# Rotary rotation of queries and keys in place, with one scratch tile in place of two

## The chip, the cores and the metric

One core of a Trainium2 chip runs the kernel. The metric is the device time of one launch in microseconds (us), the median of several. The engines are named as in the profile: PE multiplies matrices, DVE (vector), ACT (activation) and POOL (GpSimd) work element by element, SP issues transfers (DMA) from one queue, in order. PEld is the loading of PE's weights. Each engine runs its own instructions in program order, so an instruction that waits holds up all that stands behind it on its engine.

## What is computed

A backbone of two layers over 512 latent and 256 context tokens, width 1024. In each layer one input projection feeds three groups of heads: differential attention (queries and keys of 32 values per head), grouped-query attention (6 query and 2 key heads of 64) and a bidirectional gated DeltaNet with chunks of 64. An output projection and a SwiGLU follow. The change is in the rotation of the latent tokens' queries and keys, which the reference writes so:

```
def apply_axial_rope(x, cos, sin):
    xr = x.reshape(shp[0], shp[1], -1, 2, 2, nf).astype(jnp.float32)
    x1, x2 = xr[..., 0, :], xr[..., 1, :]
    c, s = cos[:, None], sin[:, None]
    out = jnp.stack([x1 * c - x2 * s, x2 * c + x1 * s], axis=-2)
```

In the DeltaNet each chunk needs the inverse of a triangular matrix (`lax.linalg.triangular_solve` in the reference). The kernel inverts 32x32 blocks element by element and puts them together with matmuls.

## The kernel before

The kernel is Python code that emits one program. A scheduler then decides in which order each engine runs its instructions, by a simulation of its own of when each would be ready; only the data dependences and the tiles' buffers are fixed. So an edit at one place can move instructions at others. An order that the code gives (`EARLY`, `PLAN` below) sets how the simulation ranks them.

Each layer begins with a projection stage. For groups of 128 tokens PE makes a product (`tps`), ACT copies it from PSUM to a slot of SBUF, and the elementwise engines work on it there. Three names matter: `gk` (a slot with the grouped-query keys and values, "kv", or queries, "gq"), `dq` (a slot with the queries and keys of the differential heads) and `rt` (scratch of the rotation; the profile calls both scratch slots of before `rt`). `rope` is called for each of the 4 latent tiles of kv, gq and dqk in both layers, 24 times: DVE multiplies by the cosine, POOL multiplies the two swapped halves by the sine (two instructions), DVE adds. All of `gk`, `gsq`, `dq`, `rt` take slots of 512 columns from one pool with 6 slots in layer 0 and 5 in layer 1:

```
PROJS = (6, 5)
EARLY = ("0 1 2 5 4 v0 q v1 3 p0 p1 q q v2",
         "0 1 2 v0 5 v1 3 q p0 4 q p1 v2 q")
INV_DVE = ((0,), (0, 2))
```

`EARLY` is the order of the code in this stage: a number prepares one tile of the DeltaNet, `q` is one of kv, gq, dqk, `vN` one inversion (`gdn_invert`, L726), `pN` what follows it for a tile (`gdn_post`, L784). An inversion is a chain of 60 small instructions on `Yg` and `Tg`, each of which needs the one before; `INV_DVE` says which run on DVE (v0 in both layers, v2 in layer 1), the others run on POOL. It loads `Yg` from `Bdram` and stores the result to `Ydram`. `gdn_post` loads that as `Z`, DVE transposes it (`ZT`), and PE merges the blocks (`mg`, L810 and L820) and goes on with `wps` and `ups`. These loads and stores stand in SP's queue, and so do the stores of the rotated tiles (`dqk<-dq`) and their loads for the attention (`gk<-dkv` and others).

Then come the mixers: attention (`S` is the score product, `nm` the row maximum on DVE, `P` the exponential on ACT, `pt` and `PT` its transpose, `pv` the product with the values), together with the DeltaNet's steps (`scan`, `ops`; `kdec` is a factor of theirs made on POOL) and further `p` stages, in the order that a table `PLAN` gives (it begins with "s0 s1 a0 a1 p2 s2" in layer 0). `gqs` and `gks` are the transposed queries and keys, `exp` the PE product that turns them. `wlo` is the rest that a weight leaves after rounding, made on DVE for the weights of a projection.

Of the kernel before, what the change touches and what calls it, by code (L numbers as in the profile page):

```python
# [94 lines left out]
class Net:  # L95
# [894 lines left out]
    def rope(self, out, x, nh, cos, sin, nf):  # L990

        d = 4 * nf
        tmp = self.slot("rt")
        tv = tmp[:, :nh * d].rearrange("p (h d) -> p h d", d=d)
        self.mul(tv, x, cos.unsqueeze(1).to_broadcast([128, nh, d]))
        t4 = self.slot("rt2")[:, :nh * d].rearrange("p (h a s f) -> p h a s f", h=nh, a=2, s=2)
        x4 = x.rearrange("p h (a s f) -> p h a s f", a=2, s=2)
        s4 = sin.rearrange("p (a s f) -> p a s f", a=2, s=2)
        for half in range(2):
            self.mul(t4[:, :, :, half], x4[:, :, :, 1 - half],  # L1000
                     s4[:, :, half].unsqueeze(1).to_broadcast([128, nh, 2, nf]), self.g)
        self.add(out, tv, t4.rearrange("p h a s f -> p h (a s f)"))

    def attn_proj(self, l):
        d = self.dram
# [568 lines left out]
def shape_consts():  # L1574
# [28 lines left out]
    for j, at in enumerate(((0, 1), (2, 3), (0, 2), (1, 3))):  # L1603
        for b in at:
            pick[:, :, j, b] = np.eye(32, dtype=f)
    return {"ident": np.eye(128, dtype=f), "pick": pick.reshape(128, 512), "masks": masks.reshape(128, 768), "mloc": mloc,
            "negm": np.concatenate([negm.reshape(128, 128), masks[:, 2:4].reshape(128, 256)], 1), "blk2": blk2,
            "rope_d": rope(32), "rope_g": rope(64)}

def layout(inp):  # L1610
# [55 lines left out]
```

## Time and profile before

| what | value |
|---|---|
| time, median of 3 runs | 2184.11 us (2183.25 to 2184.77) |
| time of the profiled execution | 2187.43 us |
| its span, first to last instruction | 2185.6 us |
| mean granted clock of PE | 0.943 of full speed |
| busy: PE, DVE, ACT, POOL | 2020.9, 1325.2, 823.8, 525.0 us |

The profiled execution took 3.3 us more than the median, and 1.8 us of its time lie outside the span. Two stretches hold the projection stages with the rotations and the start of the mixers: 190 to 420 us (layer 0) and 1390 to 1600 us (layer 1). The long stretches between are projections and the SwiGLU.

### The profile page before, as it was taken

How to read it: one execution, taken by the hardware profiler on the slowest of the kernel's cores; microseconds unless marked ns; L12 is line 12 of the kernel's file. 1: busy time of each engine (PE TensorE's matmuls, PEld its weight loads, DVE VectorE, ACT ScalarE, POOL GpSimd, SP SyncE). 2: the span in 40 equal slices, each digit the busy share in tenths (PEclk: the TensorE clock that was granted, in tenths of full speed). 3: DMA queues.
4: the chain of work that ended last, by engine and by line, in shares of the span. 5: the costliest groups of instructions: out<-in, count | busy, mean ns of one | idle time of the engine just before them, and what ended most of it. 6: DMA issues, size and time to landing. Idle time of an engine off the chain costs nothing. (4 is left out here: it accounts for less than half of the span.)

```text
span 2185.6 us, 36979 instructions
## 1 busy us (share of the span) xinstructions
PE 2020.9 (92%) x14786; PEld 1672.6 (77%) x14786; DVE 1325.2 (61%) x2223; ACT 823.8 (38%) x1609; POOL 525.0 (24%) x768
## 2 busy tenths in 40 slices
PE   7999877998889999999999989977899799999998
PEld 3788766776668888888888888865676598888887
DVE  6755774575845747565757457687767664443444
ACT  5433315464744321212122344423475653222223
POOL 2403579331014100000000350367323030000002
PEclk9999987698999999999999989987798999999999
DMA  8354434221062324343424411444212242222321
GB/s 296 121 176 132 156 109 113 47 73 35 26 227 78 116 87 154 110 131 102 155 91 140 134 56 48 133 127 125 51 47 60 86 165 77 100 85 92 106 98 61
DMA packets 167596, 236.46 MB, mean 108 GB/s; under 512 B 75328, under 2 KB 109248, under 8 KB 167424
## 3 DMA queue, kind: packets, MB, share of 16 engines
q10 hardware_dynamic: 46160, 144.92, 20.2%
q1 hardware_dynamic: 121264, 89.18, 13.4%
q8 instruction: 116, 1.90, 0.3%
q14 instruction: 56, 0.46, 0.1%
HBM read 198.00 MB, written 36.04 MB: 107 GB/s over the span
## 5 line engine op out<-in xcount | busy, mean ns | idle before, releaser
L185 ACT ACTIVATE whi<-raw 128x1024 fp32r<-128x1024 f32 (+4 forms) x246 | 220.7, 912 | 499.6 <-PE dps L188 207.3
L161 DVE TENSOR_TENSOR wlo<-raw,whi 128x1024 fp32r<-128x1024 f32 (+4 forms) x236 | 250.1, 1074 | 222.1 <-ACT whi L185 221.3
L188 PE MATMUL gu<-ahi,wlo 128*128 128x512 f32 x672 | 264.0, 393 | 1.1 <-DVE wlo L161 1.1
L188 PE MATMUL gu<-ahi,whi 128*128 128x512 f32 x672 | 263.6, 392 | 0.0
L188 PE MATMUL dps<-acth,whi 128*128 128x512 f32 (+1 forms) x560 | 186.6, 348 | 0.4 <-DVE h L179 0.2
L188 PE MATMUL dps<-acth,wlo 128*128 128x512 f32 (+1 forms) x560 | 185.7, 346 | 0.0
L188 PE MATMUL gu<-alo,whi 128*128 128x512 f32 x672 | 168.9, 392 | 0.0
L179 DVE SCALAR_TENSOR_TENSOR junk<-adaw,cb 128x1024 bf16<-128x1024 f32 x112 | 136.8, 1222 | 37.6 <-DMA adaw<-ada_t 36.6
L188 PEld LDWEIGHTS gu<-ahi,wlo 128*128 128x128 f32 x672 | 126.5, 188 | 28.3 <-DVE wlo L161 1.5
L188 PE MATMUL tps<-whi,ahi 128*128 128x512 f32 (+4 forms) x368 | 137.9, 379 | 11.1 <-ACT dq L185 7.2
L188 PEld LDWEIGHTS gu<-alo,whi 128*128 128x128 f32 x672 | 126.3, 188 | 27.6
L179 DVE SCALAR_TENSOR_TENSOR h<-dps,md,h 128x512 f32<-128x512 f32 (+1 forms) x128 | 80.6, 633 | 109.6 <-PE dps L188 109.3
L188 PEld LDWEIGHTS gu<-ahi,whi 128*128 128x128 f32 x672 | 126.5, 188 | 26.7
L188 PE MATMUL tps<-wlo,ahi 128*128 128x512 f32 (+4 forms) x368 | 138.3, 376 | 2.6 <-DVE wlo L161 2.4
L161 POOL TENSOR_TENSOR md<-md,adab 128x2 f32<-128x2 f32 x56 | 32.0, 572 | 439.5 <-DVE junk L179 439.5
L188 PE MATMUL tps<-whi,alo 128*128 128x512 f32 (+4 forms) x368 | 137.3, 373 | 0.0
L1161 DVE TENSOR_REDUCE nm<-S 128x1 f32<-128x768 f32 (+1 forms) x140 | 117.0, 844 | 32.6 <-PE S L188 31.4
L182 ACT ACTIVATE P<-S,nm 128x768 f32<-128x768 f32 (+1 forms) x140 | 114.0, 815 | 51.7 <-DVE nm L1161 46.1
L161 POOL TENSOR_TENSOR sqc<-sqc 128x256 f32<-128x256 f32 x35 | 35.4, 1012 | 397.8 <-ACT sqc L182 397.4
L188 PE MATMUL dps<-actl,whi 128*128 128x512 f32 (+1 forms) x560 | 124.3, 346 | 0.0
L188 PEld LDWEIGHTS dps<-acth,whi 128*128 128x128 f32 x560 | 105.4, 188 | 15.6 <-DVE h L179 0.4
L188 PEld LDWEIGHTS dps<-acth,wlo 128*128 128x128 f32 x560 | 105.7, 189 | 14.3
(295 smaller groups left out, 4629.0 us busy)
## 6 DMA issues: line engine op xcount, KB each, us to landing
raw<-w_u ACTq DMA_DIRECT2D x88, 512.0 KB
adaw<-ada_t ACTq DMA_DIRECT2D x56, 512.0 KB
adaw<-ada_p ACTq DMA_DIRECT2D x24, 512.0 KB
raw<-w_o ACTq DMA_DIRECT2D x24, 512.0 KB
raw<-w_d ACTq DMA_DIRECT2D x44, 256.0 KB
raw<-w_d ACTq DMA_DIRECT2D x32, 320.0 KB
adaq<-ada_q SPq DMA_DIRECT2D x16, 512.0 KB
raw<-w_t ACTq DMA_DIRECT2D x16, 512.0 KB
```

Of the source, the lines that this page charges most:

```text
L161: (eng or self.v).tensor_tensor(out=out, in0=a, in1=b, op=op)
L179: self.v.scalar_tensor_tensor(out=out, in0=a, scalar=sc, in1=b, op0=op0, op1=op1, **k)
L182: self.s.activation(out=out, in_=in_, func=func, **k)
L185: self.s.activation(out=out, in_=in_, func=AF.Copy, **k)
L188: self.t.matmul(out, lhsT, rhs, start=start, stop=stop)
L1161: self.v.tensor_reduce(out=nm, in_=pin, axis=AX.XY if nk == 768 else AX.X, op=ALU.max, negate=True)
```

## The change

`rope` takes one scratch slot. POOL writes its two sine products there first. Then DVE multiplies x by the cosine in place and adds the scratch to it. The instructions are as many as before, of the same shapes. As the cosine product overwrites what POOL reads, it now has to wait for both POOL instructions; before, it could run ahead of them or beside them.

```diff
     def rope(self, out, x, nh, cos, sin, nf):
         d = 4 * nf
-        tmp = self.slot("rt")
-        tv = tmp[:, :nh * d].rearrange("p (h d) -> p h d", d=d)
-        self.mul(tv, x, cos.unsqueeze(1).to_broadcast([128, nh, d]))
-        t4 = self.slot("rt2")[:, :nh * d].rearrange("p (h a s f) -> p h a s f", h=nh, a=2, s=2)
+        t4 = self.slot("rt")[:, :nh * d]
+        tv = t4.rearrange("p (h a s f) -> p h a s f", h=nh, a=2, s=2)
         x4 = x.rearrange("p h (a s f) -> p h a s f", a=2, s=2)
         s4 = sin.rearrange("p (a s f) -> p a s f", a=2, s=2)
         for half in range(2):
-            self.mul(t4[:, :, :, half], x4[:, :, :, 1 - half],
+            self.mul(tv[:, :, :, half], x4[:, :, :, 1 - half],
                      s4[:, :, half].unsqueeze(1).to_broadcast([128, nh, 2, nf]), self.g)
-        self.add(out, tv, t4.rearrange("p h a s f -> p h (a s f)"))
+        self.mul(x, x, cos.unsqueeze(1).to_broadcast([128, nh, d]))
+        self.add(out, x, t4.rearrange("p (h d) -> p h d", d=d))
```

With it the scheduler orders the projection stages and the mixers of both layers anew. Three places follow. A row is a line of the kernel, the operation, output and inputs, its size, and how many of the kind follow one another; numbers behind a name tell tiles apart.

PE, layer 0, before: the attention's first products and then the merge of the DeltaNet's tile 2 (p2), whose first rows are the last two.

```order
L188 MATMUL S<-gks,gqs 128x256 x2
L191 MATMUL pv<-ident,OTs 128x128
L191 MATMUL pt<-ident,P 128x128 x6
L188 MATMUL pv<-PT,gV 64x128 x6
L191 MATMUL pt<-ident,P 128x128 x3
L188 MATMUL pv<-PT,gV 64x128
L188 MATMUL S<-gks,gqs 128x256 x2
L188 MATMUL pv<-PT,gV 64x128 x5
L191 MATMUL exp<-ident,dq 128x128 x2
L810 MATMUL mg_3697<-ZT,Boff 32x32
L810 MATMUL mg_3697<-Z,Boff 32x32
```

The same place of the change:

```order
L191 MATMUL pt<-ident,P 128x128 x6
L188 MATMUL S<-gks,gqs 128x384 x8
L188 MATMUL pv<-PT,gV 64x128 x12
L191 MATMUL pt<-ident,P 128x128 x3
L810 MATMUL mg_3685<-ZT,Boff 32x32
L810 MATMUL mg_3685<-Z,Boff 32x32
```

Between the first `S` of this attention and the merge stood 38 `S`, 36 `pt`, 36 `pv` with values and 2 `exp`; now 20 `S`, 15 `pt` and 12 `pv` stand there. The other 18 `S`, 21 `pt` and 24 `pv` stand behind the merge's first rows. DVE's `ZT` and ACT's copies of this merge moved with it.

POOL, layer 0, before: the two inversions v1 (its last sizes, 96x84, 96x58 and 96x30) and v2 (its middle, 96x238 and 96x240), taken in turns, and the factors `kdec` between them.

```order
L161 TENSOR_TENSOR Yg<-Yg,Tg 96x17x14
L161 TENSOR_TENSOR Tg<-Yg 96x84
L161 TENSOR_TENSOR kdec<-tokm,sufb 64x384
L161 TENSOR_TENSOR kdec<-ident,gl 64x384
L161 TENSOR_TENSOR kdec<-tokm,sufb 64x384
L161 TENSOR_TENSOR kdec<-ident,gl 64x384
L161 TENSOR_TENSOR Tg<-Yg 96x240
L161 TENSOR_TENSOR Yg<-Yg,Tg 96x3x28
```

The same place of the change, down to the end of v1:

```order
L161 TENSOR_TENSOR Yg<-Yg,Tg 96x17x14
L161 TENSOR_TENSOR Yg<-Yg,Tg 96x3x28
L161 TENSOR_TENSOR Tg<-Yg 96x240
L161 TENSOR_TENSOR Tg<-Yg 96x58
L161 TENSOR_TENSOR Yg<-Yg,Tg 96x16x15
L161 TENSOR_TENSOR Yg<-Yg,Tg 96x2x29
L161 TENSOR_TENSOR Tg<-Yg 96x240
L161 TENSOR_TENSOR Tg<-Yg 96x30
L161 TENSOR_TENSOR Yg<-Yg,Tg 96x15x16
L161 TENSOR_TENSOR Yg<-Yg,Tg 96x30
L161 TENSOR_TENSOR Tg<-Yg 96x238
L161 TENSOR_TENSOR kdec<-tokm,sufb 64x384
```

Four `kdec` that stood ahead of v1's last instructions stand behind them.

DVE, layer 1, before: the last scaling of keys and queries, then the start of the inversion v2 (`MEMSET Yg`).

```order
L161 TENSOR_TENSOR gqs<-exp,gqs 64x512
L741 MEMSET Yg 96x32
L161 TENSOR_TENSOR Tg<-Yg 96x30
L161 TENSOR_TENSOR Yg<-Yg,Tg 96x30
L161 TENSOR_TENSOR Tg<-Yg 96x58
L161 TENSOR_TENSOR gqs<-exp,gqs 64x512
L161 TENSOR_TENSOR Yg<-Yg,Tg 96x29x2
L1161 TENSOR_REDUCE nm<-S 128x1
L161 TENSOR_TENSOR Tg<-Yg 96x84
L796 STREAM_TRANSPOSE ZT<-Z 128x768
```

The same place of the change:

```order
L161 TENSOR_TENSOR gqs<-exp,gqs 64x512 x2
L796 STREAM_TRANSPOSE ZT<-Z 128x768
L1160 TENSOR_REDUCE nm<-S 128x1
L741 MEMSET Yg 96x32
L161 TENSOR_TENSOR Tg<-Yg 96x30
L1160 TENSOR_REDUCE nm<-S 128x1
```

The second `gqs` and the transpose of p1 now stand ahead of v2's first instructions.

## Rows read from the trace of the kernel before

**Rows 1.** The page's first part: busy us, share of the span, instructions.

```profile
PE 2020.9 (92%) x14786; PEld 1672.6 (77%) x14786; DVE 1325.2 (61%) x2223; ACT 823.8 (38%) x1609; POOL 525.0 (24%) x768
```

**Rows 2.** Windows: length, then busy us of each engine, granted clock, DMA share, GB/s.

```profile
350.00:400.00 50.00, 45.95 (x652) 36.42 (x646) 25.24 (x52) 22.18 (x56) 36.82 (x65) 0.86 0.32 74
380.00:390.00 10.00, 10.00 (x126) 8.18 (x125) 1.09 (x3) 3.78 (x10) 3.17 (x9) 0.52 0.26 55
700.00:1250.00 550.00, 550.00 (x3160) 484.90 (x3161) 336.32 (x539) 127.24 (x203) 52.92 (x76) 1.00 0.37 122
1450.00:1500.00 50.00, 36.89 (x238) 28.39 (x242) 39.31 (x69) 8.23 (x19) 39.82 (x55) 0.83 0.35 110
1500.00:1550.00 50.00, 35.35 (x541) 27.91 (x540) 42.33 (x87) 24.00 (x56) 28.80 (x46) 0.80 0.53 133
```

**Rows 3.** The tile `rt`: durations in ns (least/median/most); idle us and times ahead of it.

```profile
L161 POOL TENSOR_TENSOR rt<-gk,ropeq x16: 587/804/3227, 255.1 to 1466.0; 128x192 f32<-128x192 f32 x16
...
L161 DVE TENSOR_TENSOR rt<-gk,ropek x8: 285/288/414, 203.2 to 1418.5; 128x128 f32<-128x128 f32 x8
L161 DVE TENSOR_TENSOR rt<-gk,ropeq x8: 542/544/952, 256.1 to 1458.3; 128x384 f32<-128x384 f32 x8
L161 DVE TENSOR_TENSOR rt<-dq,rope_d x8: 675/686/2559, 302.6 to 1495.2; 128x512 f32<-128x512 f32 x8
...
  POOL rt L161: 12.0, 13
```

**Rows 4.** Timeline of DVE, layer 1: start, us, instruction, idle before it and its releaser.

```profile
1461.07 0.64 DVE L161 TENSOR_TENSOR gk<-rt,rt 128x384 f32<-128x384 f32 x1 [1.03 <-POOL rt L161]
...
1463.88 1.75 DVE L161 TENSOR_TENSOR Tg<-Yg 96x238 f32<-96x238 f32 x1
```

**Rows 5.** Timeline of PE, layer 1: three of its waits.

```profile
1462.18 0.79 PE L188 MATMUL tps<-whi,ahi 128*128 128x512 f32 x1 [5.25 <-ACT dq L185]
...
1494.60 0.31 PE L810 MATMUL mg<-ZT,Boff 32*32 32x32 f32 x2 [6.48 <-DVE ZT L796]
...
1517.90 1.65 PE L188 MATMUL S<-gks,gqs 128*128 128x384 f32 x4 [4.18 <-DVE gqs L161]
```

**Rows 6.** Timeline of DVE, layer 1, from the end of v0 to the first `nm`.

```profile
1486.99 0.19 DVE L161 TENSOR_TENSOR Yg<-Yg,Tg 96x30 f32<-96x30 f32 x1
...
1493.56 0.98 DVE L796 STREAM_TRANSPOSE ZT<-Z 128x768 f32<-128x768 f32 x1 [5.18 <-DMA Z<-Ydram]
...
1515.30 1.12 DVE L161 TENSOR_TENSOR Tg<-Yg 96x30 f32<-96x30 f32 x1 [3.28 <-DMA dq<-dqk]
...
1518.14 0.96 DVE L1161 TENSOR_REDUCE nm<-S 128x1 f32<-128x768 f32 x1
```

**Rows 7.** Timeline of SP's queue, layer 1: the last two loads of p1's `Z`.

```profile
1515.14 0.86 SPq L152 DMA_DIRECT2D Z<-Ydram  x2
```

**Rows 8.** Timeline of PE, layer 0: attention and p2's merge.

```profile
333.71 1.54 PE L191 MATMUL exp<-ident,gk 128*128 128x128 f32 x6 [9.15 <-DMA gk<-dkv]
...
359.30 1.66 PE L188 MATMUL S<-gks,gqs 128*128 128x384 f32 x8
...
371.76 0.44 PE L191 MATMUL exp<-ident,dq 128*128 128x128 f32 x2
374.09 0.24 PE L810 MATMUL mg<-ZT,Boff 32*32 32x32 f32 x2 [1.89 <-DVE ZT L796]
```

**Rows 9.** Timeline of POOL, layer 0: `kdec` and the end of v1.

```profile
359.05 0.83 POOL L161 TENSOR_TENSOR kdec<-tokm,sufb 64x384 f32<-64x384 f32 x1
...
366.51 0.84 POOL L161 TENSOR_TENSOR Yg<-Yg,Tg 96x30 f32<-96x30 f32 x2
```

**Rows 10.** Timelines of SP's queue and of DVE, layer 0: from v1 to p2's transpose.

```profile
366.77 1.32 SPq L152 DMA_DIRECT2D Ydram<-Yg  x2
369.42 1.85 SPq L152 DMA_DIRECT2D Z<-Ydram  x4
...
373.06 0.98 DVE L796 STREAM_TRANSPOSE ZT<-Z 128x768 f32<-128x768 f32 x1 [4.23 <-POOL keg L161]
```

## The prediction

> **What bounds the kernel now.** I read the page's busy shares first, then windows of 50 us, then the tile `rt`, and then timelines of the places where an engine waits. PE is busy for 92% of the span and DVE for 61% [rows 1]. The windows show that this is an average over two kinds of stretch: between 700 and 1250 us PE is busy all the time at full clock, and nothing that the change touches lies there; in layer 1 between 1450 and 1550 us PE works only 36.89 and 35.35 of 50 us, and the clock granted is 0.83 and 0.80 [rows 2]. There the work is a net of chains through DVE, POOL and SP's queue. In layer 0 the like stretch ends at about 376 us: from 380 to 390 PE is busy for all of 10 us, but at 0.52 of the clock, near the lower of its two levels (1.2 GHz) [rows 2]. So a microsecond counts only where one of these chains ends last, and I take the two layers one by one.
>
> **The change itself.** It removes and adds no instruction. DVE's cosine product lasts 288 ns (keys), 544 ns (grouped queries) and 686 ns (differential heads), the median of 8 each [rows 3]. Before, it could lie beside POOL's two sine products; now it stands behind them. If DVE had nothing else to do, every rotation would end later by that product: 8 x (0.288 + 0.544 + 0.686) = 12.1 us in all, one bound. The other bound is zero, since DVE has other work in the projection stage and already waits for POOL ahead of the add (all its idle time before instructions on `rt` that POOL ends is 12.0 us in 13 places, [rows 3]); the wait only moves from the add to the product. I take 1 us in the place where DVE is saturated, the inversion v0 of layer 1, since there an idle DVE cannot be made good: 1.03 us of such a wait stand there now [rows 4], and the two products of a pair, 2 x 0.544 us, no longer fill it.
>
> The row on [rows 4] at 1463.88 also shows a multiply of 96x238 that lasts 1.75 us, and POOL's product of 128x192 has a least of 587 ns, a median of 804 and a most of 3227 [rows 3]: the two engines hold each other up when they run at once. The Trainium skill (SBUF — State Buffer, section "Who interferes with whom") states it as a rule: a DVE instruction with two inputs in SBUF and a GpSimd instruction that reads SBUF exclude each other, and the one issued second stands until the other is through. The trace agrees as far as these spreads go. By that rule a rotation's own product and halves no longer collide; it is rival D.
>
> **The slots.** A rotation now holds one slot of scratch and not two. Where the pool is short, ACT's copy out of PSUM comes sooner. The clear case is in layer 1: PE stands 5.25 us before the first product of dqk that needs the PSUM tile back [rows 5], until DVE's add at 1461.07 frees slots [rows 4]. With 5 slots, two `gk` and two `rt` leave one free, and this wait should go. But PE then comes to p0's merge sooner, and that waits 6.48 us at 1494.60 for DVE's `ZT` [rows 5]; DVE in turn has waited 5.18 us for the load of `Z` behind v0's end at 1487.2 [rows 6]. v0's own chain fixes this time. In the changed order DVE does about 1.1 us less of other work inside v0 (a reduction and part of a dq rotation), against the 1 us above. So I count the 5.25 us as swallowed: 0, with -5 as the bound should v0 end sooner after all.
>
> **Layer 1 after v0.** PE waits 4.18 us for the second `gqs` before its products `S` [rows 5]. That instruction ended late because DVE first had to start v2, whose load came at 1515.30 [rows 6]. In the new order `gqs` stands ahead of v2's start, so this `S` can start about 4 us sooner. What is late next: the first `nm`, at 1518.14 before [rows 6]. It now stands behind `ZT` of p1 (about 1 us, as the one at 1493.56, [rows 6]), which needs loads whose last two were issued at 1515.14 in 0.86 us [rows 7]. In SP's new order two of v2's loads stand behind these; I take their issue as worth twice those 0.86 us, 1.7 us, so that `ZT` may run near 1516 and `nm` near 1517, 1 us sooner than before, with its `S` pair no longer broken up by v2's start. v2 itself starts 2 to 4 us later; it is needed only several steps on. I take -3 us, nearer to the 4.18 us of `S` than to the 1 us of `nm`, since the next `S` and `nm` follow without v2 between them. Bounds: -4 if all of the wait is gained, and +3 if the loads of `Z` are late and v2 is missed after all. With the 5 us of the slots the lower bound is -9.
>
> **Layer 0.** Two moves matter. First, 24 matmuls of p1's merge now stand ahead of PE's wait of 9.15 us for the reloaded keys at 333.71 [rows 8]; they and what hangs on them run under that wait, and the attention starts about 2 us sooner. Second, p2's merge. Before, PE reached it after 371.76 + 0.44 and waited only 1.89 us [rows 8]. In the new order it stands right behind the eight `S` of 359.30, 12 `pv` and 3 `pt`. These took about 2.5 us more, so PE gets there at 359.3 + 2.5 - 2 = 360. Its `ZT` hangs on the end of v1: last `Yg` at 366.51 [rows 9], store at 366.77, load of `Z` at 369.42, `ZT` at 373.06 [rows 10] (that row blames POOL's `keg`, but the load of `Z` ends just before, too). Four `kdec` of 0.83 us [rows 9] and one or two instructions of v2 no longer stand ahead of v1's end: 4 x 0.83 + 0.6 = 3.9 us sooner, so `ZT` comes at about 369 and the merge at 370. So PE, DVE (`ZT` is in its queue as well) and ACT stand for about 10 us, and the work that filled this time before is left behind the merge. It took from 361.8 (359.3 + 2.5) to 372.2, that is 10.4 us. I take 8 us of it as work that must still be done, as the window from 350 to 400 has PE idle for 4 us of 50 [rows 2] and some of these gaps will be filled. Then the state that was reached at 374.09 comes at 370 + 8 = 378: +4 us. Bounds: if all of that work fits into later gaps, the merge's own 4 us remain as a gain (-4). If nothing fits and PE runs what is left at the lower clock, as it did in 380 to 390 us [rows 2], the 8 us become at most 8 / 0.52 = 15, and with 14 the state comes at 384: +10.
>
> **The sum.** 0 (slots) - 3 + 4 = +1 us on the profiled execution's 2187.43 us, so 2188.4; the median of the runs shown is 3.3 us lower, and on it this is 2185.1. I call a difference under 0.2% (4.4 us) no change, as a measurement of this kernel can hardly tell it. So the forecast is no change that can be told, with the two layers against each other.
>
> **The rivals.**
> A, faster: p2's early merge costs nothing, because the chains behind it (p2, then the DeltaNet's steps) and not PE's load end last in layer 0. For it: DVE and ACT are far from busy from 380 to 390 (1.09 and 3.78 of 10 us, [rows 2]). Against it: PE is busy all of these 10 us. Then layer 0 gives -4 and layer 1 -4: 2184.1 - 8 = 2176.
> B, slower: the stall at p2's merge costs all that it holds up, and the granted clock falls through it; it decides if `ZT` comes later than about 368 while PE is there at 360. Layer 0 gives +10, layer 1 nothing or little: 2184.1 + 9 = 2193.
> C, slower: the cosine product behind POOL's halves is on the path in half of the rotations, 12.1 / 2 = 6 us on top of +1: 2191. For it: v0 in layer 1 is one unbroken chain on DVE; against it: the add waited already.
> D: by the exclusion above each of the 8 rotations of grouped queries loses a collision as long as its product, 8 x 0.544 = 4.4 us; with +1 that is 2184.1 + 1 - 4.4 = 2180.7, still no change that can be told.
>
> **How the numbers follow.** Chances: the forecast 0.34, A 0.33, B 0.20, C 0.08, D 0.05. Faster is A, 0.33; no change is the forecast and D, 0.39; slower is B and C, 0.28. The range takes in A with the full -5 of the slots in part (2174) and B up to 2194. The forecast alone would lie within 2180 to 2188.
>
> **What would show it.** In the new trace: ACT's copy to `dq` in layer 1 without its wait of 5 us, and PE's wait before p0's merge longer by as much; `S` near 1518 without its wait of 4 us; v0's end in layer 1 within 1 us of its old distance from its start; in layer 0, PE waiting about 10 us for `ZT` near 360, and `kdec` behind v1's end. The prediction is wrong if PE gets to p2's merge late or `ZT` early, so that the stall is missing, or if v0 ends several microseconds sooner or later, since then the swallowed 5 us come back or p0 is late.

## The result and the profile after

The change took 2204.00 us (median of 4 runs, 2199.64 to 2209.39) against 2184.44 us before: 1.0087 of it, 95% interval 1.0071 to 1.0102. It is slower by about 19 us, outside the range given. The profiled execution has a span of 2202.9 us, 17.3 us over the one of before.

The page's first part shows that PE is busy for 0.8 us less than before [rows 1]; ACT and POOL work as long as before, and DVE is busy for 10 us more:

```profile
PE 2020.1 (92%) x14786; PEld 1672.6 (76%) x14786; DVE 1335.3 (61%) x2223; ACT 824.1 (37%) x1609; POOL 525.3 (24%) x768
```

So PE's added time went into waiting. The windows that answer to [rows 2], of the change (length, busy us of PE, PEld, DVE, ACT, POOL, granted clock, DMA share, GB/s):

```profile
350.00:400.00 50.00, 40.41 (x590) 32.28 (x591) 25.57 (x46) 21.26 (x51) 36.08 (x62) 0.86 0.35 85
380.00:390.00 10.00, 10.00 (x151) 7.80 (x146) 3.38 (x7) 5.98 (x17) 4.84 (x13) 1.00 0.21 61
1450.00:1500.00 50.00, 39.65 (x219) 32.26 (x217) 48.13 (x75) 10.67 (x22) 37.20 (x50) 0.91 0.32 107
1500.00:1550.00 50.00, 26.23 (x457) 21.74 (x459) 32.17 (x58) 19.54 (x45) 30.57 (x49) 0.66 0.50 130
```

PE lost 5.5 us of work in the window where p2's merge stands in layer 0, and 9.1 us in 1500 to 1550 in layer 1. To see which of it lasts, I compare the starts of the same work in both traces. PE's first product of the gate (`gu`) follows the mixers of a layer. In layer 0, before and then the change (timeline of PE):

```profile
689.31 0.39 PE L188 MATMUL gu<-ahi,whi 128*128 128x512 f32 x1
```

```profile
701.99 0.39 PE L188 MATMUL gu<-ahi,whi 128*128 128x512 f32 x1
```

Layer 0 has 12.7 us of the 17.3. From there to the last `S` of layer 1 the kernel before takes 1724.85 - 689.31 = 1035.5 us and the change 1742.68 - 701.99 = 1040.7: another 5.1 us. Of the 12.7 us, 2.2 were there at POOL's first rotation already (211.4 against 209.3); another execution with the same order in layer 0 reached this point at 206.2, so this part is chance.

The attention already starts late. Its first `S` on PE, before and then the change:

```profile
345.76 2.93 PE L188 MATMUL S<-gks,gqs 128*128 128x384 f32 x8
```

```profile
351.57 1.65 PE L188 MATMUL S<-gks,gqs 128*128 128x384 f32 x4 [0.46 <-DVE gqs L161]
```

Counted from POOL's first rotation this is 140.1 us against 136.5, so 3.7 us are lost before the merge is reached. More is lost behind it, as DVE shows at `O<-pv,R`, the end of an attention tile. Before, the first three and the sixth, and between them the `ZT` of p2's merge:

```profile
362.02 0.28 DVE L161 TENSOR_TENSOR O<-pv,R 128x128 f32<-128x128 f32 x1
367.88 0.28 DVE L161 TENSOR_TENSOR O<-pv,R 128x128 f32<-128x128 f32 x1
...
375.05 0.29 DVE L161 TENSOR_TENSOR O<-pv,R 128x128 f32<-128x128 f32 x1 [0.32 <-PE pv L191]
...
400.13 0.28 DVE L161 TENSOR_TENSOR O<-pv,R 128x128 f32<-128x128 f32 x1
```

The change, `ZT`, the first tile and the sixth:

```profile
370.90 0.98 DVE L796 STREAM_TRANSPOSE ZT<-Z 128x768 f32<-128x768 f32 x1 [7.93 <-DMA Z<-Ydram]
377.00 0.29 DVE L161 TENSOR_TENSOR O<-pv,R 128x128 f32<-128x128 f32 x1 [0.56 <-PE pv L191]
...
410.42 0.29 DVE L161 TENSOR_TENSOR O<-pv,R 128x128 f32<-128x128 f32 x1 [0.16 <-PE pv L191]
```

Before, two tiles were through when `ZT` came; in the change none is. The first tile is 15.0 us late, the sixth 10.3, and the last of the 30 still 10.2 (633.26 against 623.07): a third of the delay is made up, the rest stays. The DeltaNet beside it is not late at this place: `ZT` of p2 comes 2.2 us sooner than the one in [rows 10]. Its last `scan` is late in the end (513.85 against 507.12), but stands more than 100 us ahead of the attention's last `O`, so the attention ends last in the mixers.

PE's waits in the change that answer to [rows 5] and [rows 8]:

```profile
337.44 1.54 PE L191 MATMUL exp<-ident,gk 128*128 128x128 f32 x6 [6.44 <-DMA gk<-dkv]
...
371.93 0.31 PE L810 MATMUL mg<-ZT,Boff 32*32 32x32 f32 x2 [5.90 <-DVE ZT L796]
...
1513.24 0.31 PE L810 MATMUL mg<-ZT,Boff 32*32 32x32 f32 x2 [17.41 <-DVE ZT L796]
...
1529.06 3.00 PE L188 MATMUL S<-gks,gqs 128*128 128x384 f32 x8 [1.43 <-DVE gqs L161]
...
1537.06 0.28 PE L810 MATMUL mg<-ZT,Boff 32*32 32x32 f32 x2 [4.99 <-DVE ZT L796]
```

In layer 1 the 5.25 us before dq are gone and PE waits 17.41 us at p0's merge in place of 6.48; p1's merge now makes PE wait another 4.99 us, behind the first `S`. DVE stands there too, and the first `nm` behind it (DVE in the change):

```profile
1535.93 0.98 DVE L796 STREAM_TRANSPOSE ZT<-Z 128x768 f32<-128x768 f32 x1 [5.57 <-DMA Z<-Ydram]
1536.94 0.96 DVE L1160 TENSOR_REDUCE nm<-S 128x1 f32<-128x768 f32 x1
```

### The profile page after: what moved, and what is told of

It is laid out like the page before. It is cut to its first block, busy times and chain, and to the rows that moved or that the text cites. A ratio compares the mean times of both kernels' runs of the same rounds, so it can differ in the third digit from the quotient of the medians.

```text
span 2202.9 us, 36967 instructions
## 1 busy us (share of the span) xinstructions
PE 2020.1 (92%) x14786; PEld 1672.6 (76%) x14786; DVE 1335.3 (61%) x2223; ACT 824.1 (37%) x1609; POOL 525.3 (24%) x768
## 3 DMA queue, kind: packets, MB, share of 16 engines
q1 hardware_dynamic: 121264, 89.18, 13.3%
## 5 line engine op out<-in xcount | busy, mean ns | idle before, releaser
L188 PE MATMUL tps<-wlo,ahi 128*128 128x512 f32 (+4 forms) x368 | 136.5, 372 | 5.7 <-DVE wlo L161 5.5
L188 PEld LDWEIGHTS dps<-acth,whi 128*128 128x128 f32 x560 | 105.3, 188 | 15.5 <-DVE h L179 0.4
```

Source lines behind the costliest of these rows:

```text
L188: self.t.matmul(out, lhsT, rhs, start=start, stop=stop)
```

## The experiments

Three theories stood at the start. S: layer 0 loses by p2's early merge, layer 1 by its inversion v0, which POOL holds up. W: each rotation pays for its new wait. R: it is the order's chance in both layers together. Every time below is a ratio to the kernel before, run on the same chip.

**Each layer alone** (the old rotation is kept beside the new one):

```diff
+    def rope(self, *args):
+        (self.rope_one if self.lay == 0 else self.rope_two)(*args)
```

> The changed rotation in layer 0 alone, layer 1 as before. Theory S (two separate losses): layer 0's loss is the early merge of p2, which holds the attention up, and layer 1's is the inversion v0 that POOL holds up; then this kernel has about +10 us (2195) and its profile shows the first O<-pv late by 12 to 20 us against before, as the full change does, and v0 in layer 1 lasting 61 us from its first memset as before. Rival R (the scheduler's order only redistributes, and what is lost depends on chance in both layers together): the time is not the sum's part, below +4 or above +15. Rival W (each rotation pays the new wait): half of the 17 us, +8 to +9, but with DVE waits for POOL's rt as their source and no late O.

> The changed rotation in layer 1 alone, layer 0 as before. Theory S: +5 to +7 us (2190), all of it in v0 of layer 1: about 66 us from its first memset to its end instead of 61, with one instruction of 96x58 that lasts several us while POOL runs without a gap. Rival W: +8 to +9. Rival R: 0 or less.

Layer 0 alone: 2202.60 us, 1.0072 (1.0042 to 1.0102). Layer 1 alone: 2185.78 us, 1.0001 (0.9990 to 1.0012). W falls for layer 1: its rotations are half of the edit, and they cost nothing. For layer 0 this run doesn't decide on W. In the trace with layer 0 alone the first `O` is 10.0 us late, the third 15.5 and the last 13.6, and `gu` begins at 704.4. So S has the late attention of layer 0 right, though the first `O` is less late than the 12 to 20 us forecast and the total is 15 us over before and not 10. S fails for layer 1: with the edit in layer 1 alone, v0 does take 65.9 us from its `MEMSET` to its end (61.1 before, 66.6 in the change), and the layer loses nothing by it (1035.3 us from `gu` to the last `S`). R holds in part: in the trace with layer 0 alone, layer 1 takes 1043.8 us, 8.3 more than before, although its rotation is the old one.

**The pool's relief without the wait, and the wait with less relief:**

```diff
-PROJS = (6, 5)
+PROJS = (7, 6)      # with the rotation of before
+PROJS = (5, 4)      # with the rotation of the change
```

> The rotation as before with two scratch tiles, but one more slot in the pool of each layer (7 and 6 in place of 6 and 5): the relief of the pool without the new wait. Theory S, by which the order and not the wait does the harm: this kernel is reordered too, and its time moves by several us in either direction, faster only if PE's wait of 5.25 us before dq in layer 1 is not swallowed at p0's merge. I expect that wait gone, p0's merge waiting longer by as much, and a total within -3 to +6 us. Rival W: 0 or a gain of up to 5 us, since no wait was added.

> The changed rotation with one slot less in the pool of each layer (5 and 4): the new wait without the pool's relief. Theory S: another order again; the time depends on where p2's merge lands in layer 0 and what POOL runs during v0 in layer 1; anywhere from -2 to +20 us against before, and each loss is seen at one of the two places. Rival W: the full loss of 17 to 20 us stays, as the wait is the same, or grows. A rival by which the relief of the pool is itself the cause (PE runs ahead into the merges) has it near 0.

More slots for the kernel before: 2201.21 us, 1.0069 (1.0050 to 1.0088). Fewer for the change: 2211.09 us, 1.0111 (1.0090 to 1.0133). Both lie outside what S forecast: 14 us over before and not -3 to +6, and 24 us and not at most 20; for the second W had said that the loss stays or grows. The first is what counts: no wait was added, two tiles are used, and it is slower by almost as much as the change. Its layer 0 is as before (`gu` 690.2) and its layer 1 takes 14.0 us more, so neither the new wait nor a shortage of slots is the cause there. Both kernels have other orders. What they share with the change was seen when I counted, in each kernel's order on PE, the attention's `S` that stand ahead of the merges:

| kernel | `S` ahead of p2's merge, layer 0 | start of `gu` against before, us | `S` ahead of p1's merge, layer 1 | `gu` to last `S` of layer 1 against before, us |
|---|---|---|---|---|
| before | 38 | 0 | 12 | 0 |
| the change | 20 | +12.7 | 8 | +5.1 |
| layer 0 alone | 20 | +15.1 | 0 | +8.3 |
| layer 1 alone | 38 | -2.0 | 8 | -0.3 |
| slots 7 and 6 | 38 | +0.9 | 0 | +14.0 |
| in place, slots 5 and 4 | 28 | +14.0 | 0 | +12.4 |

From this a new theory, M: what costs is a merge that stands ahead of the attention's first tiles and waits for an inversion's end. It can be tried without touching the rotation.

**The merge held back in the change, and pulled forward in the kernel before.** An edge in the order, without a semaphore, keeps p2's merge on PE and DVE behind the third attention tile in the one, and the third tile behind the merge in the other. For the second, `PLAN` names p2 ahead of a1, too:

```diff
+        pe, dve = self.mark[l, LATE[l, tt]]       # third tile's last pt, its R
+        with self.tc.issue_after(pe), self.tc.issue_after(dve):
+            self.gdn_post(l, tt)
...
-PLAN = ("s0 s1 a0 a1 p2 s2 a2 ...
+PLAN = ("s0 s1 a0 p2 a1 s2 a2 ...
+        pe, dve = self.mgs[0, 2]                  # p2's first mg, its ZT
+        with self.tc.issue_after(pe), self.tc.issue_after(dve):
+            self.attend_now(l, pair, O, qts)
```

> The change, with p2's merge in layer 0 held behind the third attention tile on PE and DVE, where it stood before (36 S and 36 pt ahead of it in place of 20 and 15). Theory M (the loss in layer 0 is the attention that stands behind a merge that came too early, and it is never made up): the first O<-pv comes back from 15 us late to under 5, the first product of the gate (gu) of layer 0 from 702 to about 691, and the time falls by 8 to 12 us against the change, to 2192 to 2196; what is left is layer 1. Rival T (the attention is late because its keys and queries are): O stays 10 us late or more and the time stays near 2204. Rival G (the granted clock after the stall): gains 3 us at most.

> The kernel before, with two scratch tiles, but p2's merge put ahead of the third attention tile on PE and DVE in layer 0 (16 S and 24 pt ahead of it): the suspected cost alone, without the change. Theory M: the first three O late by 5 to 15 us as in the change, gu of layer 0 later by 7 to 13 us. Layer 1 gets another order by it, so the total is read up to gu, and is some 7 to 25 us over before. Rival T: gu within 3 us of before.

Held back in the change: 2191.25 us, 1.0013 (1.0002 to 1.0023). Pulled forward in the kernel before: 2204.97 us, 1.0070 (1.0053 to 1.0087). Both go the way that M has it. DVE in the change with the merge held: the first tile is 4.3 us late, not 15, and comes ahead of `ZT`:

```profile
366.34 0.28 DVE L162 TENSOR_TENSOR O<-pv,R 128x128 f32<-128x128 f32 x1
369.10 0.98 DVE L804 STREAM_TRANSPOSE ZT<-Z 128x768 f32<-128x768 f32 x1 [1.94 <-DMA Z<-Ydram]
372.94 0.28 DVE L162 TENSOR_TENSOR O<-pv,R 128x128 f32<-128x128 f32 x1
378.72 0.28 DVE L162 TENSOR_TENSOR O<-pv,R 128x128 f32<-128x128 f32 x1
```

PE in the kernel before with the merge pulled forward:

```profile
376.39 0.31 PE L811 MATMUL mg<-ZT,Boff 32*32 32x32 f32 x2 [10.05 <-DVE ZT L797]
```

There PE waits 10.05 us for `ZT`, where the kernel before waits 1.89 [rows 8]; the third `O` comes at 392.11 in place of 375.05, and `gu` begins 23.0 us late. With the merge held `gu` begins 5.0 late. The rows of `gu`, pulled forward and then held:

```profile
712.27 0.39 PE L189 MATMUL gu<-ahi,whi 128*128 128x512 f32 x1
```

```profile
694.36 0.39 PE L189 MATMUL gu<-ahi,whi 128*128 128x512 f32 x1
```

The sizes are not those of M. Pulled forward, `gu` was to be 7 to 13 us late and the first three `O` 5 to 15: the first two are not late at all, the third is 17.1, the sixth 10.6, and the last 21.0, so half of the 23 us is lost far behind the merge, in an order that is new there, too. Held back, `gu` was to begin at about 691 and layer 1 to keep its loss; `gu` is 5.0 us late, and layer 1 takes 5.3 us less than before.

**Layer 1's merge held too.** p1 has to be emitted in the mixers' stage for it:

```diff
-         "0 1 2 v0 5 v1 3 q p0 4 q p1 v2 q")
+         "0 1 2 v0 5 v1 3 q p0 4 q v2 q")
-        "a0 s0 s1 a1 p2 s2 s3 ...
+        "a0 a1 p1 s0 s1 p2 s2 s3 ...
+        pe, dve = self.firsts[1] if l else self.mark[l, LATE[l, tt]]   # layer 1: second row of S, its nm
+        with self.tc.issue_after(pe), self.tc.issue_after(dve):
+            self.gdn_post(l, tt)
```

> The change with both merges held: p2's in layer 0 as in the other run, and p1's in layer 1 behind 16 S and 6 pt of the attention (before: 12 S and 6 pt, in the change 8 and 0). Theory M, that the same holds in layer 1 (in the five kernels so far, none, 8 and 12 S ahead of p1's merge went with layers that cost 8 to 15, -1 to 5 and 0 us): 2182 to 2188, no slower than before. Rival V (layer 1's loss is v0, which POOL holds up): layer 1 keeps its 5 us, 2189 to 2193.

> The kernel with two scratch tiles and one more slot per pool, which took 14 us more in layer 1, with p1's merge of layer 1 held behind 16 S of the attention (none stood ahead of it). Theory M: layer 1 gives back 8 to 12 us, so 0 to +5 us against before. Rival V (the loss comes from v0, which there lasts as long as in the change): at most 3 us come back.

> The kernel before with the same two holds, so that it and the change with both holds differ by the edit alone and the merges stand alike (38 and 36 S ahead of p2's, 16 ahead of p1's). Theory M: within 5 us of before, and the two differ by under 5 us: the edit by itself is worth little. Rival E (the edit itself costs or gives): they differ by more than 5 us, either way.

> The change with p1's merge held in layer 1 only. Theory M: layer 0 keeps its loss of 10 us, layer 1 loses its own of 5: 8 to 13 us over before, about 2199 against some 2188. Rival V: layer 1 keeps its 5 us, 15 to 19 over before. Rival N (the hold helps for another reason, such as the moved code): near before.

| kernel | us | ratio (95% interval) |
|---|---|---|
| the change, both held | 2184.93 | 0.9982 (0.9971 to 0.9993) |
| before, both held | 2185.95 | 0.9983 (0.9971 to 0.9995) |
| two tiles, slots 7 and 6, layer 1 held | 2187.99 | 0.9999 (0.9987 to 1.0012) |
| the change, layer 1 held | 2197.28 | 1.0041 (1.0027 to 1.0056) |

All four totals came out as M has it: 1.0087 becomes 1.0013 with layer 0's hold, 1.0041 with layer 1's, and 0.9982 with both. The 0.69% that one more slot cost go away with layer 1's hold. With both holds the old and the new rotation take the same time, 0.9983 and 0.9982 of the kernel before. The stages in the traces say less than the totals:

| execution | order in layer 0 | first `S` after POOL's first rotation, us | start of `gu` against before, us | `gu` to last `S` of layer 1 against before, us |
|---|---|---|---|---|
| before | before | 136.5 | 0 | 0 |
| layer 1 alone | before | 135.9 | -2.0 | -0.3 |
| before, both held | before | 136.2 | +1.3 | +1.5 |
| the change | change | 140.1 | +12.7 | +5.1 |
| layer 0 alone | change | 140.3 | +15.1 | +8.3 |
| the change, layer 1 held | change | 140.1 | +11.5 | -6.8 |
| the change, layer 0 held | change, held | 140.4 | +5.0 | -5.3 |
| the change, both held | change, held | 140.8 | +6.9 | -12.7 |

Executions of one group have the same order in layer 0 (but for a few neighbouring rows on PE that start almost together), so they show what chance does: up to 4 us at `gu`, and 6.8 between the two kernels with slots 7 and 6, which also share their order there. Each row is one execution, on different chips; a few microseconds in one stage can't be told.

In layer 0 the change's order costs 13.3 us at `gu` (means of three executions each) and the hold gives back 7.1 of them, with no overlap of the groups. So p2's early merge is shown as a cause of about half of layer 0's loss. The other 6.2 us stay, most of them in the attention's start: it is about 4 us late in all five executions of the last two groups, held or not. Whether the rotation's new wait does that or the order of the projection stage, no run here separates. The hold in the kernel before moved nothing in layer 0, as the merge stood behind the third tile there already.

In layer 1 M is not shown. The change, layer 1 alone and the change with layer 0 held all have 8 `S` and no `pt` ahead of p1's merge, and v0 takes 66.6, 65.9 and 66.6 us; yet the layer takes 5.1 us more, 0.3 less and 5.3 less than before. So neither the merge's place nor v0 explains the 5.1 us, and their cause stays open. The hold takes 12.0, 14.9 and 7.4 us off layer 1 in three pairs of kernels (the change, slots 7 and 6, the change with layer 0 held) and adds 1.5 to that of before. It moved p1's code to another stage and another pool as well, so it may help by more than the order. And the kernel with the early merge in layer 0 has no `S` ahead of p1's merge, yet its layer 1 takes 3.0 us less than before.

So the equal totals with both holds are a sum of two unlike stages: `gu` 5.6 us later with the new rotation, and layer 1 14.2 us shorter. That the edit by itself is worth nothing is shown for this total, not for each layer.

**DVE beside POOL.** In the change one instruction of v0 in layer 1 lasted 4.93 us (timeline of DVE, and of POOL in the same time):

```profile
1499.75 4.93 DVE L161 TENSOR_TENSOR Yg<-Yg,Tg 96x58 f32<-96x58 f32 x1
```

```profile
1499.72 0.64 POOL L161 TENSOR_TENSOR Yg<-Yg,Tg 96x238 f32<-96x238 f32 x1
1500.32 1.61 POOL L161 TENSOR_TENSOR keg<-tokm,gex 128x384 f32<-128x384 f32 x2
1501.90 1.47 POOL L161 TENSOR_TENSOR Gm<-mloc,gt 128x768 f32<-128x768 f32 x1
1503.33 0.61 POOL L161 TENSOR_TENSOR Tg<-Yg 96x240 f32<-96x240 f32 x1
1503.90 1.39 POOL L161 TENSOR_TENSOR rt<-dq,rope_d 128x256 f32<-128x256 f32 x2
```

The DVE instruction ends inside the last of these rows, after six of POOL's instructions. The same instruction lasts 4.93 us beside the same POOL rows in two other kernels (layer 1 alone, and the change with layer 0 held). Two small kernels of their own were to show whether DVE stands through a whole row of POOL's instructions:

```python
v.tensor_tensor(out=Y[:96, :58], in0=Y[:96, :58], in1=T[:96, :58], op=ALU.mult)      # a chain of 30 on DVE
g.tensor_tensor(out=outs[i][:, :384], in0=big[:, :384], in1=big[:, 384:768], op=ALU.mult)   # 6 on POOL meanwhile
```

> A kernel of its own, which computes nothing of the reference: a chain of multiplies of 96x58 on DVE, beside POOL that in turn runs 2 and 6 products of 128x384 that don't wait for one another, 6 products of 96x240 that do, and 6 memsets; then the same 6 products beside a DVE chain with one input in SBUF, and beside one with the second input in PSUM. Theory X (a DVE instruction with two SBUF inputs stands until POOL leaves a gap): one DVE instruction lasts about as long as the whole row of 2 or 6 products (1.6 and 4.9 us), beside the dependent chain each lasts 0.3 to 0.7, beside memsets and in the last two cases 0.22 as alone. Rival (it stands for one POOL instruction at most): none lasts over 1 us.

> Again a kernel of its own that computes nothing of the reference: DVE runs the inversion's own pair of instructions (96x58, one with both inputs from one tile, broadcast, one with two tiles), beside POOL with 3 products of 128x384, 6 of 128x192 in the rotation's strided form, 6 of 128x384, and a mixed row as it stood beside the instruction of 4.93 us. Theory X2 (the shapes make DVE stand through a whole row): an instruction of 2 to 5 us in the strided or the mixed row. Rival (one POOL instruction at most, whatever the shape): none over 1.6 us, the longest product of the row.

The first, by the tile that DVE works on (ns, least/median/most, first and last start): two inputs in SBUF beside 6 products, the same beside memsets, one input in SBUF beside 6 products, second input in PSUM beside 6 products.

```profile
L25 DVE TENSOR_TENSOR Yd<-Yd,Td x25: 215/216/956, 21.8 to 32.0; 96x58 f32<-96x58 f32 x25
...
L25 DVE TENSOR_TENSOR Yd<-Yd,Td x25: 215/216/218, 48.5 to 54.5; 96x58 f32<-96x58 f32 x25
...
L27 DVE TENSOR_SCALAR Yd<-Yd x25: 188/190/975, 58.2 to 67.9; 96x58 f32<-96x58 f32 x25
...
L29 DVE TENSOR_TENSOR Yd<-Yd,q x25: 210/211/214, 71.7 to 77.6; 96x58 f32<-96x58 f32 x25
```

X falls: one DVE instruction stood through one POOL instruction (0.96 us) and no more, then the two took turns. The second kernel, with the inversion's forms, gave no `Td` or `Yf` pair over 0.85 us; its longest instruction was a one-input product of 1.39 us beside a POOL product of 1.47. Its mixed row met mostly such one-input products, so it says less than it should. Why the instruction in the change stood through six of POOL's instructions is left open. That a DVE instruction with two inputs in SBUF and a POOL instruction that reads SBUF exclude each other (956 ns in place of 216), and that a POOL memset, which only writes, does not disturb it (218 at most), agrees with the Trainium skill (SBUF — State Buffer, section "Who interferes with whom"). The page also lets a one-input product on DVE collide in a mode that uses both ports; the 975 ns agree with it, but no run here shows the mode. With the second input in PSUM none lasted over 214 ns.

## Why the prediction was wrong, step by step

- **The change itself** (1 us, bounds 0 and 12.1): in layer 1 the edit alone costs nothing (1.0001), and with both merges held the totals agree. In layer 0 it isn't settled: the attention's start is about 4 us late in every execution that has the edit there.
- **The slots** (0, the 5.25 us swallowed at p0's merge): right that the wait goes and is swallowed. But the term for v0 was mis-sized: forecast within 1 us, it lasts 66.6 us in place of 61.1, as one instruction of 96x58 stood for 4.93 us. So p0's `ZT` comes 6.0 us later, counted from `gu`. Two other kernels have the same v0 and lose nothing in layer 1, so this did not fix the total by itself.
- **Layer 1 after v0** (-3): this step failed. The second `gqs` did come ahead of v2, and PE's 4.18 us are gone. But counted from `gu` the first `S` is 4.3 us late (1529.06 in the change, 1512.07 before), as p0's merge was late. And the forecast had p1's `ZT` near 1516 and the first `nm` behind it 1 us sooner than before: DVE waits 5.57 us there for the load of `Z`, and `nm` comes at 1536.94, 6.1 us late. The layer takes 5.1 us more in this execution, not 3 less. What makes the 5.1 us is open: layer 1 alone starts its attention as late and still loses nothing.
- **Layer 0** (+4, bounds -4 and +10): the mechanism was right, the sizes were not. The merge stood where the order said, PE waited for `ZT` there, and `ZT` came at 370.9 (369 forecast, and 2.2 us are chance). Two terms failed. The attention was to start 2 us sooner; from the first rotation it starts 3.7 us later, as the reloaded keys came later (`exp` at 337.44, 333.71 in [rows 8]), so PE came to the merge at 366.0 and not 360 and waited 5.90 us, not 10. And of the work left behind, the forecast let part fit into gaps, for +4 in all; the layer lost 12.7 us in this execution (2.2 of them chance) and 13.3 in the mean of three, of which the hold gives back 7.1.
- **The sum** (+1): -3 and +4 came out as +5.1 and +12.7 in the profiled executions; what stands behind layer 1's last `S` gives back 0.5 of these 17.8 us. By the medians the edit in layer 0 alone is worth 15 us and in layer 1 alone nothing.
- **The rivals**: B named the mechanism and gave it 0.20, with +10 for layer 0, and stopped at 2193. Its second half, a granted clock that falls through the stall, does not show in layer 0: 0.86 from 350 to 400 us in both kernels, and 1.00 in place of 0.52 from 380 to 390. A fell. C falls for layer 1, where half of the rotations cost nothing; in layer 0 it is not separated. D was not tried by itself; no gain of 4 us is seen.

## What to carry to other kernels

Where a scheduler sets the order, price an edit by the order that it brings and not by its instructions alone: one more slot, with no instruction changed, cost 14 us. Look first for the point where one engine's queue joins two chains, and ask of the one that ends last how much of its work now stands behind a wait of the other. A hold on one instruction's place tells cause from company, if it is tried both ways: held back in the slow kernel and pulled forward in the fast one. Then look at the stages and not at the total alone, and compare kernels that share an order in one stage: they show how much of a difference is chance, and whether the same place costs the same twice.

## What had not been expected of the hardware

One DVE instruction of 96x58, 0.22 us by itself, stood for 4.93 us beside six of POOL's instructions, in three kernels alike, and three others in the same inversion for 1.90 to 2.02 us; in kernels of their own none stood longer than one POOL instruction. And one kernel's runs spread widely: on one chip 14 runs of before took 2180.88 to 2195.31 us, so one profiled execution is no measure of a stage to better than some microseconds.
